# A 32-byte pad at the right end of SBUF, and another place for three steps in TensorE's order

## The chip, the cores and the metric

The kernel runs on one core of one Trainium2 chip. The metric is the device time of one execution in microseconds (us), lower is better. The kernel before takes 1155.52 us (median of 3 runs, 1153.18 to 1157.91).

## What is computed

One layer of a bidirectional encoder on a sequence of 1024 tokens with 1024 channels in float32. Three mixers share one input projection, and a gated convolutional feed-forward network follows:

```
n = rmsnorm(h); proj = n @ w_in
xa, ga, ub, pc = split(proj)            # 384, 384, 384, 3*256 columns
ya = rglru(xa, ga)       # conv, 6 gate heads, forward + backward gated scans, times gelu(ga)
yb = s5(ub)              # 24 groups of 16 channels, 64 complex states each, both directions, then GLU
yc = hyena(pc)           # conv to x0, x1, v; long filter by FFT on v*x1, times x0
ymix = concat(rms(ya), rms(yb), rms(yc)) * mix_norm_g
h = h + ymix @ w_out
a, v = split(dwconv(rmsnorm(h) @ w_up)) # 2 * 2816 columns
h = h + (gelu(a) * v) @ w_down
out = rmsnorm(h)
```

## The kernel before

**Stages.** First come the norm and the 15 input projections (`ub0` to `x01`, each 128 columns wide and all 1024 tokens), with the scans of mixer A (RG-LRU) and mixer B (S5) worked in between; then the FFT convolution of mixer C (Hyena), the three products with `w_out` (tile name `wo`), the up-projection, and the down-projection (`dn`). Nearly every product is taken in three fp32r matmuls of 512 columns: each operand is held as a high and a low part, and `mm3` (L94 to L97) adds high times low, low times high and high times high.

**The up-projection** (`Ffn`) takes 22 steps j. A step makes 7 products of 512 x 512 blocks: `start(j)` two (`p<-B,A` in the trace, 24 matmuls), and `rest(j)` five (`p<-B,S`, three of `p<-T,S`, `p<-T,A`, 60 matmuls), 84 in all. The activation blocks `B11`, `B21`, `T3` and `T4` lie in the pool "pairs", those named `B22`, `T1` and `T2` in the pool "ffn1" (tag `p2`); all weight blocks (`A11` to `A22`, `S1` to `S4`) lie in "ffn1" (tags `w`, `w2`).

**Two sides of SBUF.** Pools grow from the left end, or with `side="right"` from the right end. "pairs" (activations `n`, later `B11`, `T3` and so on, and the `w_out` weights `wo`), the projections' weights ("inproj") and the residual are on the right; the slots, "ffn1", and the high and low parts `y` of mixers A and B (tag `yp`) on the left. The `y` of mixer C is in "pairs" too. By the sizes of the pools in the built program the tiles of the left start 64 bytes past a multiple of 128, those of the right 96 bytes past one.

**Order.** TensorE's order is that in which the code is written (L1444, `manual_schedule`). The other engines are ordered by a scheduler that is given the same code. In the projections, the table `before` in `program` says which work stands ahead of which half of a projection: key 2i + h is half h of projection i. Its entries are short names: `lg` is `s5.lags` (L337: sixteen small matmuls into `lk` and `k0`, an eviction on ScalarE, four small sums on VectorE and a store), `wt` is `s5.transposed` (L407: eight transposes `wtps` and two evictions `WT`), `st` is `s5.states` (L440: matmuls `S`, rotations and scans on VectorE, result `hrm`), `ou` is `s5.outputs` (L481: matmuls `Y` from `u`, from `hrm[0]` and from `hrm[1]`, L491 to L493, an eviction `ys` and a store), `lo` is `s5.load_out` (the copy `intra` and the loads `OT`), `tb` the tables of angles (L387 to L396), and `scan` is `rg_scan` (L763): four gate products of three matmuls into banks of PSUM, each evicted by ScalarE's L776, then a chain on VectorE and ScalarE (L781 to L791), with L786 and L788 on ScalarE and L785, L787, L789 and the scan L791 on VectorE. A raw projection weight has one buffer (`raw`, tag `wr`); it is loaded on SyncE's queue and split by two copies on ScalarE (L92, L94) and an adding transfer on GpSimd's queue.

PSUM has two double banks (`b2`) and four single ones (`b1`). `wtps`, `S`, `Y`, `lk`, `k0` and each gate product take single banks in turn.

Of the kernel before, what the change touches and what calls it, by code (L numbers as in the profile page):

```python
# [10 lines left out]
F32 = mybir.dt.float32  # L11
F32R = mybir.dt.float32r
AF = mybir.ActivationFunctionType
ALU = mybir.AluOpType
# [3 lines left out]
P = 128  # L18
# [87 lines left out]
def bc(ap, *shape):  # L106
    return ap.to_broadcast(list(shape))
# [505 lines left out]
class Net:  # L613
# [276 lines left out]
    def hy_signals(self, r, z):  # L890

        k = self.k
        nc, V = k.nc, k.nc.vector
        dec = k.half("dec", shape=(P, 2, 256))
        nc.sync.dma_start(dec, self.I["decay"][:, 512 * r:512 * r + 512].rearrange("p (a c) -> p a c", c=256))
        self.kz[r] = []
        for a in range(2):
            ps = k.bank("kps", (P, 2, 256))
            q = slice(64 * a, 64 * a + 64)
            w = self.w3[q, 0::2] if r == 3 else self.w3[q, 0:2]  # L900
            nc.tensor.matmul(ps, lhsT=self.hid[1][q, r::4], rhs=w, start=True, stop=True, tile_position=(64 * a, 0))
            h, l = (x.rearrange("p (s c) -> p s c", c=256) for x in (y[:, :768] for y in k.pair("p", "kz")))
            kr = k.half("kzr", shape=(P, 2, 256))
            V.tensor_tensor(kr, ps, bc(dec[:, a:a + 1], P, 2, 256), op=ALU.mult)
            k.split(h[:, 0::2], l[:, 0::2], kr, nc.gpsimd)
            zs = k.bank("zps", (P, 256))
            for c in range(2):
                nc.tensor.transpose(zs[:, P * c:P * c + P], z[c][:, 512 * a + r:512 * a + 512:4], k.ident)
            nc.scalar.activation(h[:, 1], zs, AF.Identity)
            V.tensor_tensor(l[:, 1], zs, h[:, 1].bitcast(F32), op=ALU.subtract)  # L910
            self.kz[r].append((h, l))

    def hy_table(self, m, r):
# [545 lines left out]
def program(ctx, tc, I, O, dbg=None):  # L1459
    k = K(ctx, tc)  # L1460
    nc = k.nc
# [16 lines left out]
    inproj, left, right, s5st, s5p, first, ps = (ExitStack() for _ in range(7))  # L1478
    k.open(left, "slots", s=12)
    keep = left.enter_context(tc.tile_pool(name="keep", bufs=1))  # L1480
    k.open(right, "pairs", side="right", p=8)
    k.open(inproj, "inproj", side="right", w=2)
    k.open(ps, "psum", psum=True, b2=2, b1=4)
# [71 lines left out]
    def load(src, o):  # L1555
        for i in range(src.shape[0]):
# [4 lines left out]
    lp, lg, il, tb, wt, st, lo = (s5.lag_prep, s5.lags, s5.intra_load, s5.tables, s5.transposed, s5.states,  # L1561
                                  s5.load_out)
    def later(f, b):
# [4 lines left out]
    lu, ou = lambda b: s5.load_u(b, part(ud, b)), lambda b: s5.outputs(b, part(yd, b))  # L1568
# [5 lines left out]
        7: [(lg, 0), (later, tb, 0)],  # L1574
        8: [(later, tb, 1), (lg, 1)],
        9: [(il, 0), (scan, 0, 1), (lp, 3)],
        10: [(lg, 2)],
        11: [(wt, 0), (lu, 0), (lo, 0)],
        12: [(lo, 1), (lp, 4), (lg, 3)],
        13: [(lu, 1), (st, 0), (tb, 2)],  # L1580
        15: [(wt, 1), (il, 1), (scan, 1, 1), (ou, 0)],
        16: [(lg, 4), (lp, 5)],
        17: [(tb, 3), (st, 1), (scan, 1, 0)],
        18: [(lg, 5)],
        19: [(wt, 2), (lu, 2), (lo, 2)],
        20: [(wt, 3)],
# [1 line left out]
        22: [(il, 2)],  # L1588
        23: [(tb, 4), (scan, 2, 0)],
        24: [(st, 3), (tb, 5)],  # L1590
        25: [(scan, 2, 1), (lo, 4), (wt, 4), (ou, 2)],
        26: [(lu, 4)],
        27: [(ou, 3)],
        28: [(lu, 5), (lo, 5), (st, 4)],
# [50 lines left out]
    h = [k.get("h", f"h{i}") for i in range(8)]  # L1645
# [120 lines left out]
```

## Time and profile before

| | |
|---|---|
| median of 3 runs | 1155.52 us |
| profiled execution, its own time | 1154.85 us |
| its span in the trace | 1153.1 us |
| TensorE busy | 1078.3 us, 94% of the span |
| VectorE busy | 969.8 us, 84% |
| ScalarE busy | 555.1 us, 48% |
| GpSimd busy | 296.7 us, 26% |

The span is the time from the first to the last instruction; 1.75 us of the execution's own time lie around it. The projections fill the stretch up to 275 us, the mixers and `w_out` that to about 470 us, the up-projection that to about 910 us, the down-projection the rest. A busy share is an average over these stages, so each of them has to be read by itself.

### The profile page before, as it was taken

The numbers are of one execution on the slowest core, as the hardware profiler recorded it, in microseconds if no ns is written. First come the engines' busy times: TensorE is split into PE (matmuls) and PEld (weight loads), VectorE is DVE, ScalarE is ACT, GpSimd is POOL, SyncE is SP. The second block draws the span as 40 slices with busy tenths as digits, with TensorE's granted clock in tenths as the row PEclk, the third lists the DMA queues.
The fourth block names the chain that finished last, engine by engine and source line by source line (L and its number), as shares of the span: only waits on it lengthen the run. The fifth ranks groups of instructions, "written<-read, shape, count | busy, mean of one in ns | idle before, by whom it ended". The sixth has DMA issues, their size and how long they took to land.

```text
span 1153.1 us, 13561 instructions
## 1 busy us (share of the span) xinstructions
PE 1078.3 (94%) x4970; PEld 876.4 (76%) x4970; DVE 969.8 (84%) x1283; ACT 555.1 (48%) x779; POOL 296.7 (26%) x260
## 2 busy tenths in 40 slices
PE   5899889989898899889999999999999989999897
PEld 4677678877677778668888888888888867887785
DVE  6985898997799874969989898989898799578974
ACT  6369567664143533753534343434343353545453
POOL 6021111113246341113332323232323062011001
PEclk8899989989898989989999999999999999999999
DMA  6187754447363442442322222212222861554003
GB/s 259 51 201 181 195 131 131 110 118 269 107 231 128 148 163 95 117 99 73 110 73 92 75 91 73 92 73 92 74 92 73 291 256 37 165 129 91 0 1 146
DMA packets 62830, 142.13 MB, mean 123 GB/s; under 512 B 11403, under 2 KB 19979, under 8 KB 62764
## 3 DMA queue, kind: packets, MB, share of 16 engines
q1 hardware_dynamic: 53692, 114.00, 28.9%
q0 software_dynamic: 9072, 27.27, 11.1%
q8 instruction: 39, 0.64, 0.2%
q14 instruction: 27, 0.22, 0.1%
HBM read 96.24 MB, written 30.33 MB: 110 GB/s over the span
## 4 chain that ended last, share of the span: by engine, by line
PE 57%; DVE 25%; ACT 7%; DMA 6%; issue 4%; POOL 1%; SPq 0%; POOLq 0%; DVEq 0%; ACTq 0%
PE p L97 35%; PE dn L97 12%; PE wo L97 5%; DVE dw L88 3%; DVE dr L1294 2%; DMA dr<-gd 2%; DVE G L475 1%; DVE G L473 1%; DVE h L1359 1%; DVE n L684 1%; PE ub L97 1%; DMA wgr<-in_gates 1%; DVE q L720 1%; DVE h L1110 1%; DVE prm L460 1%
## 5 line engine op out<-in xcount | busy, mean ns | idle before, releaser
L97 PE MATMUL dn<-dw 128*128 128x512 f32 x924 | 215.6, 395 | 10.7 <-DVE dw L88 10.6
L97 PEld LDWEIGHTS dn<-dw 128*128 128x128 f32 x924 | 175.0, 190 | 51.2 <-DVE dw L88 14.4
L97 PE MATMUL p<-T,S 128*128 128x512 f32 x792 | 185.7, 392 | 0.0
L97 PEld LDWEIGHTS p<-T,S 128*128 128x128 f32 x792 | 148.6, 188 | 33.5
L87 ACT ACTIVATE dw<-dr 128x512 fp32r<-128x512 f32 x154 | 88.0, 623 | 106.1 <-PE dn L97 91.9
L97 PE MATMUL p<-B,A 128*128 128x512 f32 x528 | 129.3, 400 | 0.0
L88 DVE TENSOR_TENSOR dw<-dr,dw 128x512 fp32r<-128x512 f32 x154 | 101.2, 703 | 21.7 <-ACT dw L87 21.7
L97 PEld LDWEIGHTS p<-B,A 128*128 128x128 f32 x528 | 100.0, 190 | 24.2
L97 PE MATMUL wo<-wo,y 128*128 128x512 f32 x384 | 95.6, 410 | 8.8 <-DVE ms L635 5.1
L1254 POOL TENSOR_TENSOR cv<-cv 128x1024 f32<-128x1024 f32 x22 | 78.0, 3543 | 73.5 <-DVE cv L720 60.9
L97 PEld LDWEIGHTS wo<-wo,y 128*128 128x128 f32 x384 | 75.2, 197 | 27.6 <-DVE ms L635 5.5
L1198 POOL TENSOR_TENSOR upv<-upv,upg 128x512 f32<-128x512 f32 x19 | 43.0, 2266 | 191.9 <-DVE upv L1197 191.8
L87 ACT ACTIVATE S<-upg 128x1024 fp32r<-128x1024 f32 x22 | 23.3, 1061 | 125.4 <-DVE upg L1200 119.3
L720 DVE SCALAR_TENSOR_TENSOR cv<-uv,cols,cv 128x1023 f32<-128x1023 f32 x44 | 73.4, 1668 | 0.8
L97 PE MATMUL p<-T,A 128*128 128x512 f32 x264 | 65.3, 396 | 0.0
L97 PE MATMUL p<-B,S 128*128 128x512 f32 x264 | 64.5, 392 | 0.0
L1294 DVE TENSOR_TENSOR dr<-dr 128x1024 f32<-128x1024 f32 (+1 forms) x48 | 53.1, 1127 | 8.0 <-DMA dr<-gd 8.0
L97 PEld LDWEIGHTS p<-T,A 128*128 128x128 f32 x264 | 49.5, 188 | 11.8
L97 PEld LDWEIGHTS p<-B,S 128*128 128x128 f32 x264 | 49.5, 188 | 11.8 <-DVE S L88 0.5
L720 DVE SCALAR_TENSOR_TENSOR cv<-ug,cols,cv 128x1023 f32<-128x1023 f32 x44 | 56.9, 1292 | 0.7 <-ACT cv L714 0.7
L88 DVE TENSOR_TENSOR A<-upg,A 128x1024 fp32r<-128x1024 f32 x20 | 56.8, 2841 | 0.0
L103 POOL TENSOR_TENSOR rs<-tms,c_mhalf 128x1 f32<-128x1 f32 x24 | 15.1, 631 | 121.6 <-DVE tms L651 121.5
(388 smaller groups left out, 2016.1 us busy)
## 6 DMA issues: line engine op xcount, KB each, us to landing
upg<-in_w_up SPq DMA_DIRECT2D x22, 512.0 KB, 3.3
upv<-in_w_up SPq DMA_DIRECT2D x22, 512.0 KB, 3.3
gd<-cv SPq DMA_DIRECT2D x22, 512.0 KB, 2.6
dr<-gd SPq DMA_DIRECT2D x20, 512.0 KB, 9.3
dr<-in_w_down SPq DMA_DIRECT2D x20, 512.0 KB, 8.6
x<-in_x SPq DMA_DIRECT2D x8, 512.0 KB, 7.2
dft<-in_dftf POOLq DMA_DIRECT2D x8, 512.0 KB, 9.2
wor<-in_w_out SPq DMA_DIRECT2D x8, 512.0 KB, 6.1
```

What stands on the lines that cost most here:

```text
L87: self.nc.scalar.activation(hi, raw, AF.Identity)
L88: return (eng or self.nc.vector).tensor_tensor(lo, raw, hi.bitcast(F32), op=ALU.subtract).ins
L97: mm = lambda *a, **b: self.nc.tensor.matmul(*a, **b, **kw)
L103: self.last_pow = self.nc.gpsimd.tensor_tensor(out, base, expo, op=ALU.pow).ins
L460: V.tensor_tensor(m, m, m2, op=op)
L473: V.tensor_tensor_scan(o[0:64, 1:512], r[0:64, 0:511], x[0:64, 0:511], initial=0.0, op0=ALU.mult, op1=ALU.add)
L475: V.tensor_tensor_scan(o[64:128, 510::-1], r[64:128, 511:0:-1], x[64:128, 511:0:-1], initial=0.0, op0=ALU.mult, op1=ALU.add)
L684: nc.vector.scalar_tensor_tensor(nT[1][kt][:, s], ps, self.c(gname, kt), nT[0][kt][:, s].bitcast(F32), op0=ALU.mult, op1=ALU.subtract)
L720: k.nc.vector.scalar_tensor_tensor(o[:, dst], ps[:, src], w, o[:, dst], op0=ALU.mult, op1=ALU.add)
L1198: G.tensor_tensor(a21, a21, a11, op=ALU.subtract)
L1254: G.tensor_tensor(o[0], o[0], o[1], op=ALU.mult)
L1294: self.k.nc.vector.tensor_tensor(B(o), B(x), B(y), op=f)
```

## The change

One tile of 32 bytes per partition is taken at the right end of SBUF before all other tiles of that side, so each of these starts 32 bytes lower. In the built program the tiles of the right then start 64 bytes past a multiple of 128, as those of the left do. Three entries of the table move: `lags(2)` goes from ahead of the first half of `xa1` to ahead of its second half, behind the transposes `wt(0)`; `outputs(0)` goes from ahead of the second half of `v0` to ahead of the second half of `ga1`; and ahead of the second half of `x00` the copies, the transposes `wt(4)` and `outputs(2)` now stand ahead of the gates of `scan(2, 1)`. Last, the filter's product and the split in `hy_signals` get a priority with the scheduler; the order of every engine is the same with these lines and without them.

```diff
@@ hy_signals
-            V.tensor_tensor(kr, ps, bc(dec[:, a:a + 1], P, 2, 256), op=ALU.mult)
+            with k.tc.high_priority(150):
+                V.tensor_tensor(kr, ps, bc(dec[:, a:a + 1], P, 2, 256), op=ALU.mult)
...
-            nc.scalar.activation(h[:, 1], zs, AF.Identity)
-            V.tensor_tensor(l[:, 1], zs, h[:, 1].bitcast(F32), op=ALU.subtract)
+            with k.tc.high_priority(150):
+                nc.scalar.activation(h[:, 1], zs, AF.Identity)
+                V.tensor_tensor(l[:, 1], zs, h[:, 1].bitcast(F32), op=ALU.subtract)
@@ program
+    pad = right.enter_context(tc.tile_pool(name="pad", bufs=1, side="right"))
+    pad.tile([P, 8], F32, name="pad")
     k.open(right, "pairs", side="right", p=8)
...
-        10: [(lg, 2)],
-        11: [(wt, 0), (lu, 0), (lo, 0)],
+        11: [(wt, 0), (lu, 0), (lo, 0), (lg, 2)],
...
-        15: [(wt, 1), (il, 1), (scan, 1, 1), (ou, 0)],
+        15: [(wt, 1), (il, 1), (scan, 1, 1)],
...
-        17: [(tb, 3), (st, 1), (scan, 1, 0)],
+        17: [(ou, 0), (tb, 3), (st, 1), (scan, 1, 0)],
...
-        25: [(scan, 2, 1), (lo, 4), (wt, 4), (ou, 2)],
+        25: [(lo, 4), (wt, 4), (ou, 2), (scan, 2, 1)],
```

TensorE between the halves of `v0`, before (`gate` are the products of `scan(1, 1)`, `Y` those of `outputs(0)`, `v_1416` the projection `v0`):

```order
L414 MATMUL wtps<-ident,wn 128x128 x8
L97 MATMUL gate<-ul,wg 128x512
...
L491 MATMUL Y<-u,intra 128x128
L492 MATMUL Y<-hrm,OT 128x128
L493 MATMUL Y<-hrm,OT 128x128
...
L97 MATMUL v_1416<-n_116,v0w 128x512 x3
```

The same place with the change, down to where `Y` now stands (`ga_1579` is the projection `ga1`, `S_1645` belongs to `states(1)`):

```order
L414 MATMUL wtps<-ident,wn 128x128 x8
L97 MATMUL gate<-ul,wg 128x512
...
L97 MATMUL v_1420<-n_120,v0w 128x512 x3
...
L346 MATMUL lk<-Or,s5b_577 32x128
...
L97 MATMUL ga_1579<-n_120,ga1w 128x512 x3
...
L491 MATMUL Y<-u,intra 128x128
L492 MATMUL Y<-hrm,OT 128x128
L493 MATMUL Y<-hrm,OT 128x128
...
L448 MATMUL S_1645<-u,WT 128x128 x4
```

The twelve matmuls of `Y` moved behind the second half of `v0`, the small matmuls of `lags(3)` and the first half of `ga1`. The other place of TensorE is ahead of the second half of `x00`, before:

```order
L97 MATMUL gate<-ul,wg 128x512
L97 MATMUL gate<-uh,wg 128x512 x2
...
L414 MATMUL wtps<-ident,wn 128x128 x8
L491 MATMUL Y<-u,intra 128x128
L492 MATMUL Y<-hrm,OT 128x128
L493 MATMUL Y<-hrm,OT 128x128
...
L97 MATMUL x_2216<-n_116,x00w 128x512 x3
```

And with the change:

```order
L414 MATMUL wtps<-ident,wn 128x128 x8
L491 MATMUL Y<-u,intra 128x128
L492 MATMUL Y<-hrm,OT 128x128
L493 MATMUL Y<-hrm,OT 128x128
...
L97 MATMUL gate<-ul,wg 128x512
L97 MATMUL gate<-uh,wg 128x512 x2
...
L97 MATMUL x_2220<-n_120,x00w 128x512 x3
```

The gates of `scan(2, 1)` now come last of the three, with `wtps` holding two of the four single banks and `Y` the next one. ScalarE behind the gates of that scan, before (`m` and `gt_2241` are the scan's, `Es`, `Ec` and `R` a table's, `q_2339` the projection `x00`):

```order
L714 ACTIVATE q_2339<-x_2216,cols 128x1024
L786 ACTIVATE gt_2241<-m,c_one 128x1024
L788 ACT_TABLE_LOAD
L788 ACTIVATE m<-m 128x1024
L392 ACT_TABLE_LOAD
L392 ACTIVATE Es<-ang 128x512
L393 ACTIVATE Ec<-ang 128x512
L396 ACTIVATE R<-s5rho 128x512
L430 ACTIVATE intra<-intrar 128x4x8x16
L416 ACTIVATE WT<-wtps 128x512 x2
L495 ACTIVATE ys<-Y 128x512 x2
```

And with the change:

```order
L714 ACTIVATE q_2343<-x_2220,cols 128x1024
L786 ACTIVATE gt_2281<-m,c_one 128x1024
L392 ACT_TABLE_LOAD
L392 ACTIVATE Es<-ang 128x512
L393 ACTIVATE Ec<-ang 128x512
L396 ACTIVATE R<-s5rho 128x512
L430 ACTIVATE intra<-intrar 128x4x8x16
L416 ACTIVATE WT<-wtps 128x512 x2
L495 ACTIVATE ys<-Y 128x512
L788 ACT_TABLE_LOAD
L788 ACTIVATE m<-m 128x1024
```

The table's functions, `intra`, `WT` and one `ys` moved between L786 and L788 of the scan.

## Rows read from the trace of the kernel before

**Rows 1.** The page, busy time, share of the span and count by engine

```profile
PE 1078.3 (94%) x4970; PEld 876.4 (76%) x4970; DVE 969.8 (84%) x1283; ACT 555.1 (48%) x779; POOL 296.7 (26%) x260
```

**Rows 2.** The page, the chain of waits that ended last, by line

```profile
PE p L97 35%; PE dn L97 12%; PE wo L97 5%; DVE dw L88 3%; DVE dr L1294 2%; DMA dr<-gd 2%; DVE G L475 1%; DVE G L473 1%; DVE h L1359 1%; DVE n L684 1%; PE ub L97 1%; DMA wgr<-in_gates 1%; DVE q L720 1%; DVE h L1110 1%; DVE prm L460 1%
```

**Rows 3.** Stretches: length, busy time by engine, granted clock, DMA share, GB/s

```profile
130.00:152.00 22.00, 13.60 (x62) 10.94 (x62) 21.02 (x28) 9.22 (x10) 2.50 (x10) 0.77 0.51 128
152.00:220.00 68.00, 67.92 (x382) 57.02 (x382) 61.10 (x80) 51.70 (x62) 8.87 (x28) 1.00 0.52 132
220.00:260.00 40.00, 35.12 (x180) 30.39 (x179) 39.81 (x45) 26.29 (x31) 3.79 (x15) 0.91 0.47 116
320.00:360.00 40.00, 34.94 (x162) 28.77 (x162) 39.48 (x47) 14.11 (x19) 23.07 (x15) 0.91 0.72 252
540.00:900.00 360.00, 360.00 (x1557) 291.80 (x1556) 323.35 (x319) 143.12 (x148) 118.22 (x59) 1.00 0.24 82
```

**Rows 4.** TensorE's waits from 90 to 300 us: total, times, longest

```profile
PE wtps L414 <- ACT gt L776: 4.8, 1, 4.8
PE Y L492 <- DMA intrar<-s5lag: 4.2, 1, 4.2
PE Y L493 <- DVE hrm L460: 4.0, 1, 4.0
```

**Rows 5.** VectorE's waits from 130 to 300 us

```profile
DVE prm L457 <- PE S L448: 2.3, 2, 1.8
DVE gt L781 <- ACT gt L776: 2.2, 1, 2.2
DVE gt L800 <- ACT gg L799: 1.9, 1, 1.9
DVE lks L356 <- PE k L350: 1.8, 3, 1.2
...
DVE ul L88 <- ACT uh L87: 1.2, 1, 1.2
DVE u L720 <- ACT u L714: 0.9, 1, 0.9
```

**Rows 6.** TensorE in time, one up-projection step: start us, us

```profile
607.37 5.76 PE L97 MATMUL p<-B,A 128*128 128x512 f32 x24
612.97 2.92 PE L97 MATMUL p<-B,S 128*128 128x512 f32 x12
615.73 8.44 PE L97 MATMUL p<-T,S 128*128 128x512 f32 x36
624.00 2.97 PE L97 MATMUL p<-T,A 128*128 128x512 f32 x12
626.81 5.76 PE L97 MATMUL p<-B,A 128*128 128x512 f32 x24
```

**Rows 7.** The page, a group of TensorE: busy us, mean ns of one, idle before

```profile
L97 PE MATMUL p<-T,S 128*128 128x512 f32 x792 | 185.7, 392 | 0.0
```

**Rows 8.** TensorE from 430 to 440 us (mixer B), and 450 to 460 (mixer C)

```profile
429.73 10.66 PE L97 MATMUL wo<-wo,y 128*128 128x512 f32 x45
...
449.62 10.59 PE L97 MATMUL wo<-wo,y 128*128 128x512 f32 x46
```

**Rows 9.** ScalarE in time behind the gates of `scan(2, 1)`

```profile
251.62 1.28 ACT L788 ACT_TABLE_LOAD   x1
254.24 1.06 ACT L788 ACTIVATE m<-m 128x1024 f32<-128x1024 f32 x1 [1.34 <-DVE m L787]
255.32 1.28 ACT L392 ACT_TABLE_LOAD   x1
...
260.18 1.08 ACT L495 ACTIVATE ys<-Y 128x512 f32<-128x512 f32 x2
```

**Rows 10.** Transfers issued from 195 to 262 us: KB each, us to landing

```profile
x00r<-in_w_in SPq DMA_DIRECT2D x1, 512.0 KB, 4.1
x00w<-x00r POOLq DMA_DIRECT2D x1, 512.0 KB, 5.8
```

## The prediction, made before the change was run

> **What bounds the kernel now.** I read the page's busy shares first: TensorE 94%, VectorE 84% [rows 1]. Such a share is an average, so the chain of waits comes next. Its largest pieces are TensorE in the up-projection (`p`, 35%), in the down-projection (`dn`, 12%) and in `w_out` (`wo`, 5%); the rest is mostly VectorE in small lines, among them G and q of the projections [rows 2]. The stretches then say which engine is full where [rows 3]. In the loop of the up-projection TensorE is busy 360.00 us of 360 and VectorE 323.35, so there a shorter matmul is a shorter kernel, as long as VectorE's 90% cover it. In the projections it is the other way: VectorE works 21.02 of 22 us (130 to 152), 61.10 of 68 (152 to 220) and 39.81 of 40 (220 to 260). TensorE idles for 8.4 of the first 22 us and for 4.9 of the last 40, at a mean granted clock of 0.77 and 0.91 of the upper level. So TensorE's waits there [rows 4], which the new order is about, can't be counted as gain at their face: only what VectorE stops waiting for [rows 5] can.
>
> **The pad.** It removes nothing and adds one unused tile; what it changes is where each operand of a matmul starts. One up-projection step shows what that may be worth. From one `p<-B,A` to the next it takes 626.81 - 607.37 = 19.44 us for 84 matmuls [rows 6]. Within it, start to start, the 24 of `p<-B,A` take 5.60 us (233.3 ns each), the 12 of `p<-B,S` 2.76 (230), the 36 of `p<-T,S` 8.27 (229.7), the 12 of `p<-T,A` 2.81 (234). All are the same instruction, without a wait. What differs is placement. `B,A` and `T,A` take one operand from the left side and one from the right, the two groups between have one such product in four. The same holds in `w_out`: mixer B has `y` left and `wo` right, mixer C has both on the right. With the last matmul's own 0.39 us [rows 7] taken off, mixer B needs (10.66 - 0.39) / 44 = 233.4 ns, mixer C (10.59 - 0.39) / 45 = 226.7 [rows 8]. Both operands right is as fast as this gets, so being on the right is not the fault; being offset by 32 bytes against each other is the reading that fits. The pad takes that offset away.
>
> The sum for the up-projection: at 226.7 ns, 84 matmuls take 19.04 us, 0.40 less a step. Of this 0.16 belong to `start` (5.60 against 24 x 226.7 ns = 5.44) and 0.24 to `rest`. All 22 `rest` parts count; the `start` parts of j = 0 and 1 lie beside VectorE's preparation of the blocks, so 20 count: 22 x 0.24 + 20 x 0.16 = 8.5 us. VectorE's share in the loop rises from 89.8% to 91.7%, still cover. In `w_out`, mixer B's 144 matmuls gain 6.7 ns each, 0.96 us, and are on the chain. Mixer A's 144 lie in a stretch where VectorE works 39.48 of 40 us [rows 3], so I count nothing. The products of the GLU and of the inverse FFT (150 matmuls with mixed sides, of which I find no part on the chain that is not handed on to VectorE) could give up to 150 x 6.7 ns = 1.0 us; I take 0. Pad: **9.4 us**, between 8.4 (`w_out` gives nothing) and 11.4 (mixer A and these too, 0.96 + 1.0 more).
>
> Against this stands a rule. The Trainium skill (SBUF — State Buffer, Who interferes with whom) gives TensorE two independent read ports, one for the moving operand and one for weight loads, and says that it never waits on anyone. By that rule no operand's place could slow the other, and the sum would lose its 9.4 us. The trace does not agree: 233.4 and 226.7 ns stand side by side for the same instruction. The rows decide for me, and the rule stays as rival B.
>
> **The order.** The three moves free TensorE from 4.2 + 4.0 us of waiting in `outputs(0)` (for `hrm`, whose second half VectorE had not finished; the row's name of a transfer belongs to a load that came earlier) and from 4.8 us ahead of `wt(4)` (for a gate's bank) [rows 4], 13.0 in all. The move of `lags(2)` behind `wt(0)` and the two priority lines have no row of their own that would change: 0, between -1 and +1 by the smallest waits shown [rows 5]. What counts is VectorE:
> - From 152 to 220 it idles 68 - 61.10 = 6.9 us [rows 3]. Of that 1.8 us is for `k` of `lags(3)`, which stood behind `Y` on TensorE and now stands ahead of it, and 2.2 for a gate of the next scan; both should go, since TensorE comes there 8 us earlier. 1.2 (`ul`) and 0.9 (`u`) wait for ScalarE [rows 5]; half of that may go. About 5 us.
> - After 260 us it waits 1.8 us for `S` (of the 2.3 of that row) and 1.9 for a gate of mixer A [rows 5]. Both follow TensorE and ScalarE, so I take half, 1.9 us.
> - New: on ScalarE the table's functions, `intra`, `WT` and one `ys` now stand between L786 and L788 of `scan(2, 1)`. Before, L788 began with its table load at 251.62 and ended at 255.30. The block that moved ahead ran from 255.32 to 260.18, 4.9 us [rows 9]. With it L788 would end at 251.62 + 4.9 + 1.28 + 1.06 = 258.9, 3.6 us later. Behind it on VectorE stand L789 and the scan L791, and behind these the rest of the projections. VectorE has other work for a part of that time: 3 us, between 0 and 3.6.
> - New: the gates of `scan(2, 1)` find three of four single banks taken, so each waits for ScalarE to empty the one bank. On TensorE this may cost as much as the 4.8 us that it replaces. VectorE covers it, since TensorE had 4.9 us to spare from 220 to 260 [rows 3]; without that cover it is rival C.
>
> Order: 5 + 1.9 - 3 = **3.9 us**. At the best all 6.9 + 3.7 = 10.6 go, at the worst nothing goes and the 3.6 are lost.
>
> **Forecast.** The profiled execution took 1154.85 us, its span 1153.1 with 1.75 around it; the median of the runs, 1155.52, is 0.67 higher. 1154.85 - 9.4 - 3.9 = 1141.5 us, between 1138 and 1145 if the terms are off by a few us.
>
> **The rivals.**
> A. TensorE's waits are worth their face: its 13.0 us, with some more for the clock that falls while it waits. 1154.85 - 9.4 - 13.0 = 1132, from 1129 to 1137. For it: the waits are real, and the clock was at 0.77 in that stretch. Against it: VectorE was busy 96% of the same stretch.
> B. The pad does nothing, since the slow pace comes from operands on the two sides at once, whatever their offset. 1154.85 - 3.9 = 1151, from 1148 to 1154. For it: every slow product has one operand on each side, so no row of this trace separates a side from an offset. Against it: neither side is slow in itself, and why distance alone should cost time, no row shows.
> C. The order gives nothing. The one bank of the gates holds TensorE for longer than its 4.9 us to spare, or ScalarE's L788 holds VectorE for 3.6 us. 1154.85 - 9.4 = 1145.5, down to 1149.1 with the 3.6 lost. For it: VectorE is full exactly there, so each new wait shows at once.
> D. Slower. The pad also moves the raw weights of the projections (one buffer), which then start off the boundary that they lie on now. A load takes 4.1 us and the adding transfer out of it 5.8 [rows 10], with two copies of the size of L788 (1.06 us, [rows 9]) between them: 12 us a weight, and the next load waits for the end. Should both transfers take twice as long, 22 us a weight, a weight would take 4 us longer than a projection does (six of them, `v0` to `x00`, from 152 to 260 us: 18 us each). For about eight weights: 1154.85 - 9.4 + 32 = 1177. It is slower than before once a weight takes 6 + 9.4 / 8 = 7.2 us more. Against it: the adding transfer's 5.8 us are for writing to just such an offset, and twice that is far.
>
> That the change doesn't do what it says is B for the pad, and holds for the priority lines in any case (no order changes with them: 0).
>
> **How the numbers follow.** Forecast 0.58; A 0.10; B 0.08; C 0.21; D 0.03. The likeliest gives 1141.5 us. For 8 in 10 the range leaves out D, most of B and the lower part of A: 1135.5 to 1149.5. A measurement of this kernel tells about 0.5%, 5.8 us, from no change: faster than 1149.7 us are the forecast, A, C and a little of B, 0.89; within it lies the rest of B, 0.08; D is slower, 0.03.
>
> **What would show it.** In the profile after, a step of the up-projection should take 19.04 us and all four groups 226.7 to 227 ns a matmul; mixer B's `wo` too. At 19.44 rival B holds. VectorE's idle time from 152 to 220 us should fall from 6.9 to about 2; if its waits for `k` and for the gate are there as before, the order's term is wrong. A new wait of L789 for ScalarE of 2 to 4 us near 250 should appear, and TensorE's wait for L776 should come up at the gates instead of at `wtps`. The first `p` should start about 4 us earlier. If TensorE's 13 us arrive there in full, A is right; if it starts no earlier, C.

## The result and the profile after

| | before | after |
|---|---|---|
| median of 4 runs each | 1156.59 us | 1141.96 us |
| range | 1153.18 to 1157.91 | 1140.53 to 1144.42 |
| profiled execution, its own time | 1154.85 us | 1140.53 us |
| its span | 1153.1 us | 1138.7 us |

The ratio is 0.9876, 95% interval 0.986 to 0.9893: faster by 1.2%. Two further comparisons of the same two kernels gave 0.9888 (0.9865 to 0.991) and 0.99 (0.988 to 0.992). The forecast was 1141.5 us.

Where the 14.3 us of the two profiled executions come from is read by setting the start of the same work side by side (the times stand in the timelines of TensorE):

| TensorE begins or ends | before, us | after, us | lead |
|---|---|---|---|
| first `kps` (projections done) | 275.20 | 270.35 | 4.9 |
| first `wo` | 331.33 | 325.89 | 5.4 |
| last matmul of `wo` | 466.40 | 460.19 | 6.2 |
| `start(2)`, first of the gapless `p` | 499.72 | 493.39 | 6.3 |
| first `dn` | 918.41 | 904.84 | 13.6 |
| end of the span | 1153.1 | 1138.7 | 14.3 |

Half of it lies in the up-projection. The table sets one execution against one; the five traces in which the table `before` is untouched have their first `kps` between 274.56 and 276.55 us, the three of the changed kernel between 270.35 and 272.87. One step of it after the change, TensorE in time (start us, us, line, tiles, count), to be held against [rows 6]:

```profile
600.20 5.60 PE L97 MATMUL p<-B,A 128*128 128x512 f32 x24
605.64 2.88 PE L97 MATMUL p<-B,S 128*128 128x512 f32 x12
608.36 8.32 PE L97 MATMUL p<-T,S 128*128 128x512 f32 x36
616.52 2.88 PE L97 MATMUL p<-T,A 128*128 128x512 f32 x12
619.24 5.60 PE L97 MATMUL p<-B,A 128*128 128x512 f32 x24
```

A step takes 619.24 - 600.20 = 19.04 us instead of 19.44, and all four groups go at one pace: 5.44 / 24, 2.72 / 12, 8.16 / 36 and 2.72 / 12 are 226.7 ns each. Mixer B's `w_out` follows (425 to 435 us; mixer C, 445 to 455 us, is as it was in [rows 8]):

```profile
424.80 10.36 PE L97 MATMUL wo<-wo,y 128*128 128x512 f32 x45
...
444.78 10.59 PE L97 MATMUL wo<-wo,y 128*128 128x512 f32 x46
```

The stretches of the projections, columns as in [rows 3]:

```profile
130.00:152.00 22.00, 20.05 (x114) 16.00 (x112) 21.63 (x28) 12.51 (x14) 3.40 (x11) 1.00 0.53 125
152.00:220.00 68.00, 64.96 (x348) 55.26 (x349) 66.48 (x86) 47.83 (x59) 7.88 (x27) 0.95 0.58 144
220.00:260.00 40.00, 34.67 (x176) 28.64 (x176) 33.85 (x38) 31.71 (x38) 3.77 (x15) 0.91 0.51 139
```

VectorE, the third pair of numbers, works 66.48 us of the 68 where it had 61.10. From 220 to 260 it is the other way: 33.85 of 40 where it had 39.81. TensorE is busy 20.05 of the first 22 us (13.60 before), at a granted clock of 1.00 of the upper level, which had been 0.77 on average while it waited for `hrm`. What the two engines wait for, TensorE from 90 to 300 us and VectorE from 130 to 300:

```profile
PE gate L97 <- ACT gt L776: 7.3, 5, 3.8
PE zps L909 <- DVE kzr L905: 3.7, 2, 2.3
PE Y L491 <- DVE lks L356: 2.1, 1, 2.1
PE gate L97 <- ACT ys L495: 0.9, 1, 0.9
```

```profile
DVE gt L789 <- ACT m L788: 4.8, 2, 4.6
DVE kz L912 <- ACT kz L911: 1.4, 1, 1.4
DVE q L720 <- ACT q L714: 1.1, 1, 1.1
DVE prm L457 <- PE S L448: 0.8, 2, 0.5
```

The waits of [rows 4] are gone; five shorter ones for L776 stand at the gates, and one for `ys`. Of VectorE's waits in [rows 5] hardly one is left (`lks` 0.2, `prm` 0.8), and one has come: L789 for L788, 4.6 us in one piece. [rows 5] leaves out the longest wait of its window, 2.7 us for the load `Oi` ahead of 130.61 us; it stands after the change too, 2.4 us ahead of 129.19 us.

### The profile page after: what moved, and what is told of

It reads as the page before. It is cut to its first block, busy times and chain, and to the rows that moved or that the text cites. A ratio compares the mean times of both kernels' runs of the same rounds, so it can differ in the third digit from the quotient of the medians.

```text
span 1138.7 us, 13553 instructions
## 1 busy us (share of the span) xinstructions
PE 1069.6 (94%) x4970; PEld 876.5 (77%) x4970; DVE 969.0 (85%) x1283; ACT 554.4 (49%) x778; POOL 296.5 (26%) x260
## 4 chain that ended last, share of the span: by engine, by line
PE 39%; DVE 7%; DMA 3%; issue 1%; POOL 0%; ACT 0%; POOLq 0%; SPq 0%; ACTq 0%
PE p L97 27%; PE dn L97 12%; DVE dw L88 3%; DVE dr L1296 2%; DMA dr<-in_w_down 2%; DMA dr<-gd 2%; DVE h L1361 1%; DVE A L88 0%; DVE cv L720 0%; POOL upg L1201 0%; DVE h L1368 0%; DVE S L88 0%; DVE upg L1202 0%; ACT S L87 0%; DVE h L1377 0%
## 5 line engine op out<-in xcount | busy, mean ns | idle before, releaser
L97 PE MATMUL p<-T,S 128*128 128x512 f32 x792 | 183.1, 389 | 0.0
L720 DVE SCALAR_TENSOR_TENSOR cv<-uv,cols,cv 128x1023 f32<-128x1023 f32 x44 | 73.4, 1668 | 0.8
L720 DVE SCALAR_TENSOR_TENSOR cv<-ug,cols,cv 128x1023 f32<-128x1023 f32 x44 | 56.9, 1292 | 0.7 <-ACT cv L714 0.7
```

The source lines that it names most:

```text
L97: mm = lambda *a, **b: self.nc.tensor.matmul(*a, **b, **kw)
L720: k.nc.vector.scalar_tensor_tensor(o[:, dst], ps[:, src], w, o[:, dst], op0=ALU.mult, op1=ALU.add)
```

## Experiments

**The pad alone.** No engine's order differs from before.

```diff
+    pad = right.enter_context(tc.tile_pool(name="pad", bufs=1, side="right"))
+    pad.tile([P, 8], F32, name="pad")
```

> The kernel before with the 32-byte pad on the right alone; no engine's order changes. Theory (the offset of 32 bytes between the two operands costs the time): a step of the up-projection takes 19.04 us instead of 19.44, w_out of mixer B 226.7 ns a matmul; the time falls by 8.4 to 9.4 us, ratio about 0.992, and up to the first p of the gapless stretch little moves. Rival (pad and order only work together, or the gain of the up-projection comes from an earlier start): the ratio stays above 0.996.

Measured: 1147.70 us against 1155.54, ratio 0.9929 (0.9904 to 0.9954). TensorE in time, one step:

```profile
602.43 5.60 PE L97 MATMUL p<-B,A 128*128 128x512 f32 x24
...
621.47 5.60 PE L97 MATMUL p<-B,A 128*128 128x512 f32 x24
```

19.04 us. The first `kps` starts at 274.56 us, 0.6 earlier than before, and from `start(2)` to the first `dn` the lead grows by 7.9 us. So the pad works without the order, and where it was said to. The profiled execution, 1143.02 us, was the fastest of the four, so the 11.9 us by which its span is shorter are more than the 7.8 between the medians.

**The order alone.** The three moves in the table, without the pad.

> The kernel before with the three moves in the table alone, no pad. Theory: steps of 19.44 us as before; the projections end 3 to 5 us earlier (first kps at about 271 instead of 275.2 us), and this lead lasts to the end: ratio 0.996 to 0.9975. Rival (TensorE's waits of 13 us count in full): first kps 10 us earlier or more, ratio below 0.991. Rival (nothing): 275 us and a ratio of 1.

Measured: 1148.32 us against the same 1155.54, ratio 0.9939 (0.992 to 0.9959). Steps take 19.44 us (622.36 - 602.92), the first `kps` starts at 270.67 us as expected. The time fell further than expected: 7.0 us by the ratio, 4.7 to 9.2 by its interval, where 3 to 5 were awaited. The profiled execution, 1150.21 us, was the slowest of the four, so its trace (4.6 us of lead at the end) is at the lower end too. VectorE was busy 66.60 us of 152 to 220, with the same wait of 4.6 us at L789. Pad and order together, 7.1 and 6.1 thousandths, come to 13.2; the changed kernel had 12.4, 11.2 and 10.0 in its three comparisons. Within the intervals they add up.

**The other side moved.** The pad at the left end in place of the right.

```diff
+    lpad = ctx.enter_context(tc.tile_pool(name="lpad", bufs=1))
+    lpad.tile([P, 8], F32, name="lpad")
     k.open(left, "slots", s=12)
```

> The kernel before with 32 bytes on the left side instead of on the right, so that the tiles of both sides start 96 bytes past a multiple of 128. Offset theory: operands are level again, a step takes 19.04 us, 226.7 ns for all groups, about 1146 us. Rival (an operand must start on a multiple of 64): now nothing does, steps of 19.44 us or more. Rival (operands on both sides at once are slow): 19.44 us, about 1155 us.

Measured: 1147.05 us (one run). TensorE in time:

```profile
606.05 5.60 PE L97 MATMUL p<-B,A 128*128 128x512 f32 x24
...
625.09 5.60 PE L97 MATMUL p<-B,A 128*128 128x512 f32 x24
```

19.04 us. Every tile now starts 96 bytes past a multiple of 128, none on a multiple of 64, and four of a step's seven products still have their operands on two sides. Both rivals fall: neither a boundary that an operand must start on, nor the two sides, make the slow pace.

**Both sides moved.** Both pads at once, 32 bytes each.

> The kernel before with 32 bytes on the left and 32 on the right: both sides move, the left to 96 bytes past a multiple of 128, the right to 64. Offset theory: the operands are 32 bytes apart again, steps of 19.44 us as before, about 1155 us. Rival (any pad on the right gives the gain, by where the right side starts): 19.04 us, 1147 us.

Measured: 1156.30 us (one run). TensorE in time:

```profile
608.77 5.76 PE L97 MATMUL p<-B,A 128*128 128x512 f32 x24
614.37 2.91 PE L97 MATMUL p<-B,S 128*128 128x512 f32 x12
617.11 8.43 PE L97 MATMUL p<-T,S 128*128 128x512 f32 x36
625.38 2.96 PE L97 MATMUL p<-T,A 128*128 128x512 f32 x12
628.18 5.76 PE L97 MATMUL p<-B,A 128*128 128x512 f32 x24
```

19.41 us: the tiles of the right start where they do in the changed kernel, and the gain is gone, since the left has moved off them. It is the place of one operand against the other.

**A pad of 96 bytes on the right** (`[P, 24]` in place of `[P, 8]`), for how near "level" has to be.

> The kernel before with a pad of 96 bytes on the right: its tiles start on multiples of 128, those of the left 64 bytes past one. If the offset counts by 64, it is zero: steps of 19.04 us, about 1146 us. If it counts by 128, half of it is left: steps of 19.44 us, about 1155 us, or in between.

Measured: 1155.82 us (one run). TensorE in time:

```profile
609.00 5.76 PE L97 MATMUL p<-B,A 128*128 128x512 f32 x24
614.60 2.90 PE L97 MATMUL p<-B,S 128*128 128x512 f32 x12
617.34 8.42 PE L97 MATMUL p<-T,S 128*128 128x512 f32 x36
625.60 2.96 PE L97 MATMUL p<-T,A 128*128 128x512 f32 x12
628.40 5.76 PE L97 MATMUL p<-B,A 128*128 128x512 f32 x24
```

19.40 us; `p<-B,A` at 5.60 / 24 = 233.3 ns as with an offset of 32. An offset of 64 bytes costs as much, so being level within 64 bytes is not enough. Level within 128 was enough in the changed kernel and with the left pad; whether a larger multiple plays a part was not tried.

**outputs(0) alone with the pad.**

```diff
-        15: [(wt, 1), (il, 1), (scan, 1, 1), (ou, 0)],
+        15: [(wt, 1), (il, 1), (scan, 1, 1)],
...
-        17: [(tb, 3), (st, 1), (scan, 1, 0)],
+        17: [(ou, 0), (tb, 3), (st, 1), (scan, 1, 0)],
```

> Pad and the move of outputs(0) alone. Theory (this move carries the order's gain, since it lets lags(3) and the gates of the next scan come 8 us earlier on TensorE and so ends VectorE's waits for them; lags(2) is worth nothing): as with both moves, 1139 to 1142 us, VectorE busy about 66 us from 152 to 220. Rival (lags(2) is half of it): 1143 to 1146 us.

Measured: 1141.38 us against 1154.69, ratio 0.9884 (0.9866 to 0.9902); the changed kernel on the same chip 1144.19, ratio 0.99. One move of the three gives all that the three give together. VectorE from 152 to 220 us:

```profile
152.00:220.00 68.00, 64.45 (x353) 55.02 (x354) 66.57 (x86) 47.83 (x59) 7.88 (x27) 0.97 0.59 145
```

66.57 us, as in the changed kernel.

**The third move alone with the pad** (`wt(4)` and `outputs(2)` ahead of the gates of `scan(2, 1)`), and **both others without it**.

```diff
-        25: [(scan, 2, 1), (lo, 4), (wt, 4), (ou, 2)],
+        25: [(lo, 4), (wt, 4), (ou, 2), (scan, 2, 1)],
```

> Pad and only the third move (wt(4) and outputs(2) ahead of the gates). Theory: the 8 us of TensorE's waits for hrm near 140 stay, VectorE's idle time from 152 to 220 stays near 7 us, and the wait for L788 comes on top: no gain over the pad alone or a loss of up to 3 us, 1146 to 1150 us. Rival: the third move carries the order's gain, 1142 us.

> Pad and the moves of lags(2) and outputs(0), but ahead of x00's second half the old order (gates, copies, wt(4), outputs(2)). Theory (the 4.8 us of TensorE ahead of wt were covered by VectorE, so that this move brought no gain and one new wait): as fast as the changed kernel or up to 3 us faster, 1139 to 1142 us, with TensorE's wait for L776 at wtps back. Rival (the third move is worth its 4.8 us): 1145 to 1147 us.

Measured, on one chip with the changed kernel: the third move alone 1151.10 us, ratio 0.9953 (0.9931 to 0.9974), so less gain than the pad alone had on another chip (0.9929) and 1 us slower than expected; the other two without it 1139.96 us, ratio 0.9865 (0.984 to 0.989); the changed kernel 1143.21 us, ratio 0.9888. Waits of VectorE with the third move alone:

```profile
DVE gt L789 <- ACT m L788: 5.6, 1, 5.6
DVE lks L356 <- PE k L350: 2.6, 3, 2.0
DVE gt L781 <- ACT gt L776: 2.2, 1, 2.2
```

The waits for `k` and for the gate, which `outputs(0)` takes away, are there as before, and L789 waits 5.6 us on top. With both others and without the third move TensorE waits again at `wtps`, and the time is no longer for it:

```profile
PE wtps L414 <- ACT gt L776: 5.8, 2, 3.7
```

So the third move takes 4.8 us of waiting from TensorE, which did not count. VectorE gets 4.6 us at L789, but without the third move it waits nearly as long a little later:

```profile
259.52 0.69 DVE L457 TENSOR_TENSOR prm<-S,Ec 128x512 f32<-128x512 f32 x1 [3.08 <-PE S L448]
261.56 1.22 DVE L800 TENSOR_TENSOR gt<-gt,gg 128x1024 f32<-128x1024 f32 x1 [1.35 <-ACT gg L799]
```

By medians the third move costs about 3 us; the intervals of the two overlap, but the three pairs (with and without it beside both others, alone beside the pad, and the changed kernel beside outputs(0) alone) point the same way. That the new wait is this cost is not shown. At the first `kps` the profiled executions differ by less than 1 us: 272.87 us in the changed kernel against 272.12 without the third move, and 272.79 against 272.48 with outputs(0) alone (at 84 us, ahead of all moved work, the changed kernel was 1.8 us late in the first pair and 0.4 early in the second). At the last matmul of `wo` they differ by 4.5 and 3.4 us, although behind 262 us every engine has the same order with the third move as without it. What sets those later microseconds stays open.

**Another order for the third move.** Outputs first, then the gates, the transposes last.

```diff
-        25: [(lo, 4), (wt, 4), (ou, 2), (scan, 2, 1)],
+        25: [(lo, 4), (ou, 2), (scan, 2, 1), (wt, 4)],
```

> The changed kernel again, on the chip of the next three, as their measure: ratio to before 0.986 to 0.990, about 1142 us, with VectorE's wait of about 4.6 us for L788 and TensorE's waits of about 7 us at the gates as before.

> The changed kernel with another order ahead of the second half of x00: copies, outputs(2), gates of scan(2, 1), and the transposes wt(4) last. Theory (wt ahead of the gates holds two banks, and lets the table's functions in between L786 and L788): the gates' waits fall from 7.3 to at most 3 us, the 4.6 us wait of VectorE for L788 goes, and since VectorE was held by it, the kernel is 2 to 4.5 us faster than the changed one: 1138 to 1140 us. Rival (VectorE's wait there is covered by something later, such as the weights or the last gate): the wait goes, and the time stays within 1 us.

Measured: the changed kernel 1143.21 us (6 runs, 1140.73 to 1146.65), this one 1139.37 us (6 runs, 1136.93 to 1142.99), ratios to before 0.9888 (0.9865 to 0.991) and 0.9857 (0.9833 to 0.9881). Waits of both engines in the new one:

```profile
PE gate L97 <- ACT gt L776: 5.5, 3, 2.9
...
PE gate L97 <- ACT ys L495: 1.7, 1, 1.7
```

```profile
DVE gt L800 <- ACT gg L799: 0.3, 1, 0.3
DVE gt L789 <- ACT m L788: 0.2, 1, 0.2
```

VectorE's wait at L789 is gone (0.2 us), and `kps` starts at 268.12 us instead of 272.87 (2.1 of these 4.8 us were there at 84 us, ahead of all moved work). The waits at the gates fell only to 7.2 us in all, not to 3 as expected: four products still share few banks. That `kps` comes earlier all the same shows again which engine counts there. Both were run once more on the same chip, in another comparison:

> Once more the changed kernel with outputs(2), gates and then wt(4) ahead of x00's second half: 1138 to 1141 us, 2 to 4.5 us below the changed kernel on the same chip.

> Once more the changed kernel, as the measure of the run with outputs first: 1141 to 1144 us.

Measured: 1140.94 us (1139.14 to 1141.75), ratio 0.9875 (0.9857 to 0.9893), against 1144.19 us (1141.16 to 1144.73), ratio 0.99 (0.988 to 0.992). Again the lower median is that of outputs first, by 3.3 us, so this version beats both kernels by its medians in two comparisons; the intervals of the two still overlap. `kps` starts at 268.46 us against 272.79, and here nothing of it was there at 84 us.

Leaving the third move out altogether gives nearly the same time (1139.96 beside 1139.37, and 1141.38 with outputs(0) alone beside 1140.94), although its `kps` starts 4.0 us later (272.12 for 268.12). The lead of outputs first does not last: it is 4.1 us at the first `wo`, 1.0 at the last. In between TensorE waits longer for VectorE. From 320 to 470 us, first with outputs first, then without the third move:

```profile
PE wo L97 <- DVE ms L635: 6.7, 1, 6.7
PE wo L97 <- DVE wo L1045: 5.5, 2, 3.2
```

```profile
PE wo L97 <- DVE ms L635: 5.2, 1, 5.2
...
PE wo L97 <- DVE wo L1045: 1.2, 2, 1.0
```

With outputs first the scheduler also ordered VectorE's work behind 320 us differently. Whether that makes these waits was not tried.

## Why the prediction held, point by point

**The total** lay within half a microsecond of the forecast (1141.96 for 1141.5), and so near a hit is luck: by themselves the pad measured 8.2 us for 9.4 and the order 7.0 for 3.9, and the two further comparisons had 1143.21 and 1144.19 us.

**The pad's mechanism** held to the digit: 19.04 us a step, 226.7 ns in all groups, mixer B's `wo` at (10.36 - 0.39) / 44 = 226.6 ns. That it is the operands' offset was read from two pairs of rows; the left pad and the two pads together show it. The same matmuls take 233.3 or 226.7 ns by the place of their operands alone. The rule weighed ahead of it (the Trainium skill, SBUF — State Buffer, Who interferes with whom, by which TensorE's two read ports are independent and TensorE never waits on anyone) speaks of engines in each other's way; taken as the prediction took it, that no operand's place could slow the other, these runs go against it, and the measurement decides.

**The pad's size** was put at 8.5 us in the up-projection; from `start(2)` to the first `dn` the lead grew by 13.6 - 6.3 = 7.3. The sum's 20 starts and 22 rests are right; what it left out is that a faster TensorE meets its inputs at the loop's beginning:

```profile
494.26 7.12 PE L97 MATMUL p<-B,A 128*128 128x512 f32 x23 [0.40 <-DMA A<-upg]
...
529.16 2.81 PE L97 MATMUL p<-B,S 128*128 128x512 f32 x11 [0.36 <-DVE S L88]
```

These two waits are 0.76 of the missing 1.2 us. With the pad alone, where the loop begins 3 us later and only the second of these waits stands, the lead grew by 7.9. In `w_out` the sum booked 0.96 us: from the first to the last matmul of `wo` the lead grew by 0.8 here, and by 2.3 with the pad alone (135.07 us before, 132.77 with it). So more counted there in one order than in the other; why is not shown. The whole pad, 9.4 us by the sum, measured 1155.54 x (1 - 0.9929) = 8.2, 5.3 to 11.1 by the interval.

**The order's sum**, 5 + 1.9 - 3 = 3.9 us, came out near what the waits of this trace give because two mis-sized terms offset each other. From 152 to 220 VectorE's idle time fell from 6.9 to 1.5 us: 5.4 for 5. After 260 the waits for `S` and for the gate of mixer A went almost whole (0.5 us for `S`, none at L800): about 3.2 for 1.9. The new wait was put at 3 us, 3.6 at the most, and was 4.6. ScalarE in time, against [rows 9]:

```profile
246.31 1.14 ACT L786 ACTIVATE gt<-m,c_one 128x1024 f32<-128x1024 f32 x1
247.47 1.28 ACT L392 ACT_TABLE_LOAD   x1
...
252.26 0.59 ACT L495 ACTIVATE ys<-Y 128x512 f32<-128x512 f32 x1
252.88 1.28 ACT L788 ACT_TABLE_LOAD   x1
254.17 1.06 ACT L788 ACTIVATE m<-m 128x1024 f32<-128x1024 f32 x1
```

VectorE's last `q` (L720) ahead of it, before and then after, and L789 after:

```profile
254.13 1.27 DVE L720 SCALAR_TENSOR_TENSOR q<-x,cols,q 128x1023 f32<-128x1023 f32 x1
```

```profile
249.37 1.28 DVE L720 SCALAR_TENSOR_TENSOR q<-x,cols,q 128x1023 f32<-128x1023 f32 x1
...
255.26 1.23 DVE L789 TENSOR_TENSOR gt<-gt,m 128x1024 f32<-128x1024 f32 x1 [4.61 <-ACT m L788]
```

The block between L786 and L788 took 247.47 to 252.85, 5.4 us, half a microsecond more than the 4.9 taken; and VectorE, which was expected to have other work in between, ran out of it. The step that failed is the bound: it counted how much later L788 would be than before, not what VectorE would have left to do by then. L788 ended when it had before (255.23 us for 255.30), while VectorE's last `q` ahead of L789 started 4.8 us earlier; the wait took back nearly all of that. Together 5.4 + 3.2 - 4.6 = 4.0, less the 1.1 us that VectorE now waits for L714. The 3.2 and the 4.6 hang together: without the third move VectorE still waits 3.1 us for `S` and 1.4 at L800, and does not wait at this L789.

By time the order is worth 7.0 us alone (4.7 to 9.2), and on top of the pad, by the ratios, 0.9929 - 0.99 to 0.9929 - 0.9876 of 1155.5 us: 3.4 to 6.1 us. The 4.9 us of lead at `kps` hold 1.5 that were there at 83 us, ahead of all moved work, in this execution; in two other profiled executions of the changed kernel the lead at `kps` was 2.3 and 2.4 us. Whether the order is worth more than 3 to 6 us stays open.

**The gates through one bank.** The stall came as foreseen, at the gates instead of at `wtps`: 3.8 + 0.8 + 0.8 us for `scan(2, 1)`. It cost TensorE what the stall at `wtps` had cost: the first half of `x00` starts 5.2 us earlier than before (217.23 for 222.44), the second half 5.1 (236.57 for 241.70). That the whole third move is no gain the sum did not say outright; it holds no gain for the 4.8 us and charges 3.

**The rivals.** A (TensorE's waits at their face): TensorE's three waits are gone, 13.0 us, and the projections ended 4.9 us earlier, but 8.2 us of new waits came at the gates, so this alone does not decide. The kernel without the third move does: from 90 us to the first `kps` TensorE idles 14.7 us, before it was 14.8, and yet this `kps` comes 3.1 us earlier; VectorE's idle time there fell from 26.8 to 24.2. So A is out. B (the two sides): out by the left pad. C (the order gives nothing): out for the three moves together, and true for the third move, which brings no gain. D (slower weight loads): the load of `x00` landed after 4.1 us and the transfer out of it after 5.9, as in [rows 10].

```profile
x00r<-in_w_in SPq DMA_DIRECT2D x1, 512.0 KB, 4.1
x00w<-x00r POOLq DMA_DIRECT2D x1, 512.0 KB, 5.9
```

The moves of `lags(2)` and the priority lines were put at nothing: with outputs(0) alone the kernel is as fast as with both moves (0.9884 and 0.9865), and the traces of the changed kernel and of the three moves without the priority lines show every engine in the same order.

## What to carry to other kernels

Where the same matmul shows two paces in a trace, set out where each operand starts before looking for a wait: here 32 bytes at either end of SBUF were worth 0.7%, and 32 at both ends nothing. Price a reordering by the idle time of the engine that is full in that stretch, not by the waits of the one that isn't, and look at what the scheduler does with the queues that were not meant: the third move freed TensorE and put a block of ScalarE's work in front of the one result that VectorE needed. Follow a lead to the end of the kernel before counting it: 4.0 us at the end of the projections were 1.0 at the end of `w_out`. A bound for a new wait needs both sides, how late the result comes and how much other work the waiting engine still has.

## What the runs showed of the hardware that was not expected

- With fp32r operands of 512 columns, a matmul takes 226.7 ns from start to start when its two operands start at the same place within 128 bytes (64 and 64, or 96 and 96), and 233.3 to 234.2 ns when they lie 32 or 64 bytes apart (5.60 / 24 and 2.81 / 12, before). Other offsets were not tried, nor why it is so.
- A product of level operands that follows a product of unlevel ones is slow at first: `p<-B,S` takes 2.76 / 12 = 230 ns before, 2.74 / 12 = 228 with both pads, 2.74 / 12 = 228 with the pad of 96 bytes, and 226.7 once everything is level. Before, the first seven matmuls from 612.97 us on start 224 to 241 ns apart, the last five 226 to 227.
- VectorE's total shows nothing of it: busy 969.8 us before and 969.0 after over the same 1283 instructions.
- The granted clock fell with TensorE's waits and came back without them: 0.77 before and 1.00 after from 130 to 152 us, 1.00 and 0.95 from 152 to 220 us (busy 67.92 and 64.96 of 68), 0.91 in both from 220 to 260 us, where the waits moved from `wtps` to the gates.
